# A hybrid decoder layer on one core: convolution sides in parts, attention chunks in three steps, PSUM banks of the output projection in turn, matmuls on a tile of ones at the start

## The chip, the cores and the metric

The kernel runs on one core of a Trainium2 chip. The metric is the device time of one execution in microseconds (us), compared as medians of runs. TensorE (PE) multiplies, VectorE (DVE) and ScalarE (ACT) do the elementwise work, GpSimd (POOL) takes a few reciprocal roots, SyncE's queue (SP) issues nearly all loads and stores.

## What is computed

One layer of a hybrid decoder on 2048 tokens behind 16 learned meta tokens, width 1024, in float32:

```python
s = layer_norm(concat([meta, x]), ln_in_g, ln_in_b)
u = s @ w_in          # columns: conv value, conv gate, q, k, v, r, g_down
c_val, c_gate, q, k, v, r, g_down = split(u)
h = c_val * sigmoid(c_gate)
conv_out = silu(layer_norm(causal_depthwise_conv(h, conv_w, width=31) + conv_b))
log_g = log_sigmoid(g_down @ gate_up + gate_bias) / 16
o = gla_chunked(q, k, v, log_g)     # 4 heads, chunks of 64, state S
gla_out = rms_norm(o, gla_norm_g) * silu(r)
mix = concat([conv_out, gla_out]) @ w_out
s = layer_norm(alpha * s + mix)
s = layer_norm(alpha * s + square(relu(s @ w_ff1)) @ w_ff2)
return s[:, 16:]
```

## The kernel before

The 2048 tokens go through in four sub-sequences of 512 (`NSUB`), each held as four tiles of 128 (`TT`). Every product of float32 matrices is three matmuls of a high and a low part in fp32r (L387-L389, L465-L467, L863-L865, L1013-L1015, L1241-L1243); the splits are a cast on ACT (L190) and a subtraction on DVE (L191).

**Stages.** `win_units(0..3)` project one sub-sequence each with `w_in` (to about 572 us of the profiled execution): gate and value of the convolution, v, the gate's low-rank part (`gd_unit`), r, then two units of K and two of Q. `wout_units(0)` and `(1)` follow to about 720 us, then the two feed-forward products of the first half of the tokens: FF1 (`w1`, to about 1040 us) and FF2 (`w2`, to about 1350 us), both with seven products in place of eight, so that blocks of weights and activations are first added on DVE (L984, L1057, L1191). `wout_units(2)` and `(3)` and the same two products for the second half make up the rest. FF2 writes some added blocks to DRAM (`td<-wr`) and reads them back (`wr<-td`).

**What sets the order.** `Program` holds a list of units, each with an estimated cost. Work beside the units is a generator (a side) with a number of steps, a first and a last unit: `emit` advances it by the share of the cost gone by, and finishes it at its last unit. A scheduler then lays each engine's instructions in order by priority; `later(gen, 100)` lowers that of the convolution, so that its instructions fill gaps. In the trace each engine starts its instructions in that order.

**Convolution.** `conv(s)` loads 512 channels in four blocks (`hin`), starts each on ACT (L720) and adds 30 taps on DVE (L723, one instruction per tap, 480 in all); then for each 128 tokens it transposes (L730), normalises (L732-L742), transposes back (L747), multiplies (L755) and stores to DRAM (`mixd<-cy`, L756). `mix_load(s)` later loads that back (`mraw<-mixd`, L828) and splits it for `wout_units(s)`. Before, `conv(2)` spans from the projections of sub-sequence 3 to the start of FF2, and `conv(3)` lies within FF2.

**Attention.** `gla(s)` runs in seven steps per chunk of 128 tokens: scores (L655, L657), masked copy (L661), state update and output (L667-L680), squares (L687) and their root (L214 on DVE, L215 on POOL), the scaled product `og` with r (L696), four transposes of `og` on PE (L701), copy (L703), store (L704).

**Output projection.** `wout_units` makes two passes of 512 columns, each over four PSUM tiles for the four tiles of 128 tokens: two of the pool `gl` (two banks), two of `mm` (four banks). DVE adds each to `wacc` (L870), which is loaded by `acc_load` (L836).

**End.** The last product of FF2 adds each tile to its sum (`acc1`, L1212), then squares (L240), normalises (L250, L252) and stores.

## Time and profile before

| what | value |
|---|---|
| median of 3 runs | 2082.47 us (2079.40 to 2083.93) |
| profiled execution | 2085.16 us, of which the span 2083.4 us |
| mean granted TensorE clock | 0.992 |
| PE busy | 2022.4 us, 97% |
| DVE busy | 1600.7 us, 77% |
| ACT busy | 1031.5 us, 50% |
| POOL busy | 83.8 us, 4% |
| DMA | 409 MB, 196 GB/s over the span |

The profile is one execution; its times count from the start of the span. Busy time overlaps on PE, because matmuls are pipelined: an instruction of 0.39 us can start 0.23 us after the one before it. A view of waits names an engine, the line that waited, and the instruction that released it.

### The profile page before, as it was taken

The numbers are of one execution on the slowest core, as the hardware profiler recorded it, in microseconds if no ns is written. First come the engines' busy times: TensorE is split into PE (matmuls) and PEld (weight loads), VectorE is DVE, ScalarE is ACT, GpSimd is POOL, SyncE is SP. The second block draws the span as 40 slices with busy tenths as digits, with TensorE's granted clock in tenths as the row PEclk, the third lists the DMA queues.
The fourth block names the chain that finished last, engine by engine and source line by source line (L and its number), as shares of the span: only waits on it lengthen the run. The fifth ranks groups of instructions, "written<-read, shape, count | busy, mean of one in ns | idle before, by whom it ended". The sixth has DMA issues, their size and how long they took to land.

```text
span 2083.4 us, 26276 instructions
## 1 busy us (share of the span) xinstructions
PE 2022.4 (97%) x9144; PEld 1649.9 (79%) x9144; DVE 1600.7 (77%) x2570; ACT 1031.5 (50%) x1774; POOL 83.8 (4%) x97
## 2 busy tenths in 40 slices
PE   7999999999989999999999999999999999999998
PEld 5878778888877878778888788878788788888886
DVE  6699899989997677665598999669877654744776
ACT  4453483554543466555653433545655555444332
POOL 2000000101000000000000000002000000000001
PEclk9999999999999999999999999999999999999999
DMA  6533434434345656654799968367666546965772
GB/s 210 176 98 107 138 112 119 155 104 122 95 149 179 204 189 213 216 187 157 253 337 384 316 233 289 101 213 229 226 222 207 190 149 240 356 225 189 245 246 79
DMA packets 245861, 409.39 MB, mean 196 GB/s; under 512 B 21488, under 2 KB 115920, under 8 KB 245728
## 3 DMA queue, kind: packets, MB, share of 16 engines
q1 hardware_dynamic: 226720, 368.91, 53.8%
q10 hardware_dynamic: 19008, 38.81, 4.9%
q8 instruction: 72, 1.18, 0.2%
q14 instruction: 61, 0.50, 0.1%
HBM read 297.29 MB, written 110.35 MB: 196 GB/s over the span
## 4 chain that ended last, share of the span: by engine, by line
PE 52%; DVE 23%; DMA 14%; issue 4%; ACT 4%; SPq 1%; POOL 1%; ACTq 0%; DVEq 0%; POOLq 0%
DVE cacc L723 8%; PE mm L1241 7%; PE mm L1242 7%; PE mm L1243 7%; DMA w1r<-in_w_dram 5%; PE mm L1013 5%; PE mm L1014 4%; PE mm L1015 4%; DVE wsl L191 2%; DMA lr<-hor 2%; DVE op L191 2%; PE mm L388 2%; PE mm L387 2%; PE mm L389 2%; PE gl L1015 1%
## 5 line engine op out<-in xcount | busy, mean ns | idle before, releaser
L723 DVE SCALAR_TENSOR_TENSOR cacc<-hin,sm,cacc 128x512 f32<-128x512 f32 x480 | 345.1, 744 | 2.7 <-ACT cacc L720 0.9
L190 ACT CAST wsl<-raw 128x512 fp32r<-128x512 f32 x224 | 136.6, 620 | 174.9 <-PE mm L467 53.5
L1242 PE MATMUL mm<-op 128*128 128x512 f32 x544 | 212.5, 391 | 1.6 <-DVE op L191 1.6
L1241 PE MATMUL mm<-op 128*128 128x512 f32 x544 | 212.4, 391 | 0.2 <-DVE ac L1254 0.2
L1243 PE MATMUL mm<-op 128*128 128x512 f32 x544 | 212.2, 390 | 0.0
L190 ACT CAST op<-wr 128x1024 fp32r<-128x1024 f32 x92 | 92.2, 1049 | 210.5 <-PE mm L1243 148.4
L191 DVE TENSOR_TENSOR wsl<-raw,wsl 128x512 fp32r<-128x512 f32 x224 | 150.7, 684 | 29.5 <-ACT wsl L190 29.0
L191 DVE TENSOR_TENSOR op<-wr,op 128x1024 fp32r<-128x1024 f32 x92 | 108.6, 1218 | 69.5 <-ACT op L190 69.4
L191 DVE TENSOR_TENSOR wop<-w1r,wop 128x512 fp32r<-128x512 f32 x152 | 103.2, 687 | 70.6 <-ACT wop L190 69.5
L1013 PE MATMUL mm<-x,wop 128*128 128x512 f32 x384 | 151.7, 396 | 5.3 <-ACT u L1073 4.2
L387 PE MATMUL mm<-xt,wsl 128*128 128x512 f32 x384 | 153.7, 400 | 1.9 <-DVE r L522 1.9
L1014 PE MATMUL mm<-x,wop 128*128 128x512 f32 x384 | 150.7, 392 | 0.6 <-DVE x L191 0.6
L388 PE MATMUL mm<-xt,wsl 128*128 128x512 f32 x384 | 151.2, 394 | 0.0
L389 PE MATMUL mm<-xt,wsl 128*128 128x512 f32 x384 | 150.8, 393 | 0.0
L1015 PE MATMUL mm<-x,wop 128*128 128x512 f32 x384 | 150.4, 392 | 0.0
L191 DVE TENSOR_TENSOR op<-lr,op 128x1024 fp32r<-128x1024 f32 (+1 forms) x96 | 105.1, 1129 | 22.7 <-ACT op L190 22.6
L1242 PEld LDWEIGHTS mm<-op 128*128 128x128 f32 x544 | 102.1, 188 | 23.9 <-DVE op L191 2.8
L1241 PEld LDWEIGHTS mm<-op 128*128 128x128 f32 x544 | 102.1, 188 | 21.8 <-DVE ac L1254 0.6
L1243 PEld LDWEIGHTS mm<-op 128*128 128x128 f32 x544 | 102.1, 188 | 21.4
L190 ACT CAST wop<-w1r 128x512 fp32r<-128x512 f32 x152 | 92.8, 619 | 47.0 <-DVE w1r L984 23.6
L1013 PE MATMUL mm<-xt,wop 128*128 128x512 f32 x256 | 100.7, 396 | 2.9 <-ACT a L1063 2.8
L1013 PE MATMUL gl<-x,wop 128*128 128x512 f32 x256 | 101.4, 396 | 0.0
(278 smaller groups left out, 4781.8 us busy)
## 6 DMA issues: line engine op xcount, KB each, us to landing
wr<-in_w_dram SPq DMA_DIRECT2D x120, 512.0 KB, 6.3
lr<-hor SPq DMA_DIRECT2D x104, 512.0 KB, 6.1
raw<-in_w_in_dram SPq DMA_DIRECT2D x160, 256.0 KB, 3.0
w1r<-in_w_dram SPq DMA_DIRECT2D x64, 512.0 KB, 4.6
wr<-td SPq DMA_DIRECT2D x40, 512.0 KB, 5.5
raw<-in_w_out_dram SPq DMA_DIRECT2D x64, 256.0 KB, 3.8
hor<-s SPq DMA_DIRECT2D x64, 256.0 KB, 3.7
raw<-in_w_dram SPq DMA_DIRECT2D x40, 256.0 KB, 3.9
```

The source lines that it names most:

```text
L190: nc.scalar.copy(hi, src)
L191: (eng or nc.vector).tensor_tensor(out=lo, in0=src, in1=hi.bitcast(F32), op=ALU.subtract)
L387: nc.tensor.matmul(ps, wh, mov(k, 0), start=(k == 0), stop=False)
L388: nc.tensor.matmul(ps, wh, mov(k, 1), start=False, stop=False)
L389: nc.tensor.matmul(ps, wl, mov(k, 0), start=False, stop=(k == KD - 1))
L723: nc.vector.scalar_tensor_tensor(out=acc, in0=h[:, j:j + SUB], scalar=wc(j), in1=acc, op0=ALU.mult, op1=ALU.add)
L1013: nc.tensor.matmul(ps, wh, X[i][:, k, 0, :], start=start and k == 0, stop=False, skip_group_check=not start)
L1014: nc.tensor.matmul(ps, wh, X[i][:, k, 1, :], start=False, stop=False, skip_group_check=not start)
L1015: nc.tensor.matmul(ps, wl, X[i][:, k, 0, :], start=False, stop=(k == 3), skip_group_check=not start)
L1241: nc.tensor.matmul(ps, lh, rt[n][:, p, 0, :], start=(q == 0 and p == 0), stop=False)
L1242: nc.tensor.matmul(ps, lh, rt[n][:, p, 1, :], start=False, stop=False)
L1243: nc.tensor.matmul(ps, ll, rt[n][:, p, 0, :], start=False, **ends)
```

## The change

Six edits:

1. A tile of ones and 22 bf16 matmuls of 128x512 on it stand ahead of the first transposes.
2. `conv(2)` and `conv(3)` are one chain of steps: 49 between the start of `wout_units(0)` and the start of FF1, 148 from 24 units into FF1 to the start of FF2, 99 within FF2.
3. `gla` has three steps per chunk, and the transposes, the copy and the store of a chunk's `og` are issued in the first step of the next chunk (`turn`).
4. The passes of `wout_units` take their PSUM tiles by turns as `ggmm`, `mmgg`, `mmmm`.
5. In the projections of sub-sequence 3, `mix_load(0)` is added between the two Q units and no longer ahead of the K units.
6. The last `acc1` of the second half has a higher priority.

```diff
 from contextlib import ExitStack
+from itertools import chain
 import numpy as np
...
             s.finish()
+def part(gen, n):
+    for _ in range(n):
+        try:
+            next(gen)
+        except StopIteration:
+            return
+        yield
 @with_exitstack
 def hymba_kernel(ctx: ExitStack, tc: tile.TileContext, x, meta, ln_in_g, ln_in_b, w_in, small, gate_up,
                  w_out, ln1_g, ln1_b, w1, w2, ln2_g, ln2_b, out):
...
     nhalf = cpool.tile([P, NH], F32, name="nhalf")
     nc.vector.memset(nhalf, -0.5)
     sm = cpool.tile([P, SM_N], F32, name="sm")
+    ones = cpool.tile([P, P], BF16, name="ones")
+    nc.vector.memset(ones, 1.0)
+    wm = glp.tile([P, 512], F32, tag="gl", name="gl").rearrange("p (a c) -> p a c", a=4)
+    for _ in range(22):
+        nc.tensor.matmul(wm, ones, ones.rearrange("p (a c) -> p a c", a=1).broadcast_to([P, 4, P]), start=True, stop=True)
     s0d = [[dp.tile([P, D], F32, name=f"s0d{s}_{t}") for t in range(TT)] for s in range(NSUB)]
     hd = [[dp.tile([P, HALO + SUB], F32, name=f"hd{s}_{c}") for c in range(CT)] for s in range(NSUB)]
...
         w.gd = prog.mark()
         prog.add(gd_unit, cost=4.5)
         tok_units(C_R, r_evac, True)
+        for u in ch_units(C_K, k_evac, km_evac if s == 0 else None):
+            prog.add(*u)
+        qu = ch_units(C_Q, q_evac)
+        prog.add(*qu[0])
         if s == NSUB - 1:
             prog.add(lambda: mix_load(0), cost=0.01)
-        for u in ch_units(C_K, k_evac, km_evac if s == 0 else None):
-            prog.add(*u)
-        for u in ch_units(C_Q, q_evac):
-            prog.add(*u)
+        prog.add(*qu[1])
     def gla(s):
         w = W[s]
+        out_ = [None]
+        def turn():
+            if out_[0] is None:
+                return
+            og, lo = out_[0]
+            tp = tp_tile()
+            for h in range(NH):
+                nc.tensor.transpose(tp[:, h * P:(h + 1) * P], og[:, h * P:(h + 1) * P], ident)
+            go = pa.tile([P, 512], F32, tag="go", name="go", bufs=1)
+            nc.scalar.activation(go, tp, AF.Identity, scale=sm[:, SM_GG:SM_GG + 1])
+            nc.sync.dma_start(out=mixd[s][1][:, :, lo:lo + P], in_=go.rearrange("p (h t) -> p h t", h=NH))
+            out_[0] = None
         for c in range(TT):
             a = gl_tile().rearrange("p (h c) -> p h c", h=NH)
             lo, hi = c * P, c * P + CH
...
                                  start=True, stop=True)
                 nc.tensor.matmul(a[:, 2 * p:2 * p + 2, CH:], w.kx[p][:, lo:lo + P], qbd[p][:, :, hi:hi + CH],
                                  start=True, stop=True)
-            yield
+            turn()
             ats = at[c % 2]
             nc.vector.copy_predicated(ats, msk.bitcast(I32).rearrange("p (a c) -> p a c", a=1)
                                       .broadcast_to([P, NH, P]), a)
...
             for h in range(NH):
                 nc.tensor.matmul(o[:, h * P:(h + 1) * P], ats[:, h, :], w.v[c][:, h * P:(h + 1) * P],
                                  start=False, stop=(h == NH - 1))
-            yield
             for p in range(2):
                 for h in range(2):
                     rows, cols = slice(h * 64, (h + 1) * 64), slice(h * P, (h + 1) * P)
                     nc.vector.scalar_tensor_tensor(out=sout[rows, p, cols], in0=sin[rows, p, cols],
                                                    scalar=w.e[p].dt[rows, c:c + 1], in1=ds_[rows, p, cols],
                                                    op0=ALU.mult, op1=ALU.add)
-            yield
             og = pa.tile([P, 512], F32, tag="og", name="og")
             ss = stp.tile([P, NH], F32, tag="ss", name="ss")
             for h in range(NH):
...
                 sl = slice(h * P, (h + 1) * P)
                 nc.vector.scalar_tensor_tensor(out=og[:, sl], in0=o[:, sl], scalar=rr[:, h:h + 1],
                                                in1=w.r[c][:, sl], op0=ALU.mult, op1=ALU.mult)
-            yield
-            tp = tp_tile()
-            for h in range(NH):
-                nc.tensor.transpose(tp[:, h * P:(h + 1) * P], og[:, h * P:(h + 1) * P], ident)
-            go = pa.tile([P, 512], F32, tag="go", name="go", bufs=1)
-            nc.scalar.activation(go, tp, AF.Identity, scale=sm[:, SM_GG:SM_GG + 1])
-            nc.sync.dma_start(out=mixd[s][1][:, :, lo:lo + P], in_=go.rearrange("p (h t) -> p h t", h=NH))
-            yield
-
-    GLA_N = TT * 7
+            out_[0] = (og, lo)
+            yield
+        turn()
+        yield
+    GLA_N = TT * 3 + 1
     hdone = set()
...
             a = wacc[s, tt] = B.w.tile([P, D], F32, tag="wacc", name="wacc", bufs=4)
             nc.sync.dma_start(out=a, in_=s0d[s][tt])
+    turns = [0]
     def wout_units(s, late=None):
         sums = {}
...
             def unit(k, c=c, ls=ls, st=st):
                 if k == 0:
-                    st.ps = [gl_tile() if tt < 2 else mm_tile() for tt in range(TT)]
+                    st.ps = [(gl_tile if x == "g" else mm_tile)() for x in ("ggmm", "mmgg", "mmmm")[turns[0] % 3]]
+                    turns[0] += 1
                 wsl = prog.slot[ls[k]]
                 for tt in range(TT):
                     xh = xs(mx[s], k, 0)[:, tt * P:(tt + 1) * P]
...
                 add(x.slot[5], x.slot[5], x.slot[7])
             else:
                 o, to = {2: (x.c[:, 0], x.sa[:, 0:1]), 3: (x.c[:, 1], x.sa[:, 1:2]), 4: (x.c[:, 2], x.sb[:, 0:1])}[i]
-                acc1(o, o, ps, 1.0, to)
+                with tc.high_priority(offset=60 if half and i == 4 else 0):
+                    acc1(o, o, ps, 1.0, to)
                 if half and i == 4:
                     for _ in ln2(3, tt):
                         pass
...
     prog.side(gla(NSUB - 1), GLA_N, m_wout - 1, m_wout)
     prog.side(later(conv(0), CONV_LATE), CONV_N, W[0].gv_end, bounds[1] + 16)
     prog.side(later(conv(1), CONV_LATE), CONV_N, W[1].gv_end, bounds[3])
-    prog.side(later(conv(2), 100), CONV_N, W[3].gv_end, m_f20)
-    prog.side(later(conv(3), 100), CONV_N, m_f20, m_w2 - 4)
+    both = chain(later(conv(2), 100), later(conv(3), 100))
+    n_a, n_b = CONV_N // 3, CONV_N
+    prog.side(part(both, n_a), n_a, m_wout + 2, m_ff0 - 6)
+    prog.side(part(both, n_b), n_b, m_ff0 + 24, m_f20)
+    prog.side(both, 2 * CONV_N - n_a - n_b, m_f20, m_w2 - 4)
     prog.side(ln2_sub(0), 3 * TT, m_w2, m_w3)
     prog.side(ln2_sub(1), 3 * TT, m_w3, m_ff1)
     prog.emit()
```

Line numbers of the changed kernel are higher: L214 is L231 there, L191 is L208, L696 is L728, L680 is L713, L723 is L751, L1191 is L1223, L756 is L784, L787 is L815, L828 is L856, L836 is L864.

On DVE, in the projections of sub-sequence 1, where `og` of the third chunk of `gla(0)` is made, there stands before (`rr` is the root of the mean square, `wsl` and `xt` are splits for the projection):

```order
L191 TENSOR_TENSOR wsl<-raw,wsl 128x512
L191 TENSOR_TENSOR xt<-tp,xt 128x4x128 x2
L214 TENSOR_SCALAR rr<-ss 128x4
L723 SCALAR_TENSOR_TENSOR cacc<-hin,sm,cacc 128x512
L696 SCALAR_TENSOR_TENSOR og<-gl,rr,r 128x128
L723 SCALAR_TENSOR_TENSOR cacc<-hin,sm,cacc 128x512
L191 TENSOR_TENSOR wsl<-raw,wsl 128x512
L723 SCALAR_TENSOR_TENSOR cacc<-hin,sm,cacc 128x512
L696 SCALAR_TENSOR_TENSOR og<-gl,rr,r 128x128
```

and in the changed kernel:

```order
L713 SCALAR_TENSOR_TENSOR S_279<-S_278,dt,gl 64x128 x4
L231 TENSOR_SCALAR rr<-ss 128x4
L208 TENSOR_TENSOR wsl<-raw,wsl 128x512
L208 TENSOR_TENSOR xt<-tp,xt 128x4x128 x2
L728 SCALAR_TENSOR_TENSOR og<-gl,rr,r 128x128 x4
L751 SCALAR_TENSOR_TENSOR cacc<-hin,sm,cacc 128x512
L208 TENSOR_TENSOR wsl<-raw,wsl 128x512
L751 SCALAR_TENSOR_TENSOR cacc<-hin,sm,cacc 128x512 x3
```

The four L696 stand together, without taps between them. On PE the four transposes that read them were one by one between the matmuls; they are one group now, whose first stands 57 matmuls later.

On DVE in FF2 of the first half, from the third sum `wr<-wr` of added blocks on (`op` and `ox` are split operands, of loads `wr` and `lr`), there stands before:

```order
L1191 TENSOR_TENSOR wr<-wr 128x1024
L191 TENSOR_TENSOR op<-wr,op 128x2x512 x2
L191 TENSOR_TENSOR op<-lr,op 128x2x512 x2
L723 SCALAR_TENSOR_TENSOR cacc<-hin,sm,cacc 128x512
L1191 TENSOR_TENSOR wr<-wr 128x1024
L723 SCALAR_TENSOR_TENSOR cacc<-hin,sm,cacc 128x512 x7
L191 TENSOR_TENSOR ox<-wr,ox 128x2x512 x2
L191 TENSOR_TENSOR op<-lr,op 128x2x512 x2
L723 SCALAR_TENSOR_TENSOR cacc<-hin,sm,cacc 128x512
L1191 TENSOR_TENSOR wr<-wr 128x1024
L723 SCALAR_TENSOR_TENSOR cacc<-hin,sm,cacc 128x512
```

and in the changed kernel:

```order
L1223 TENSOR_TENSOR wr<-wr 128x1024
L208 TENSOR_TENSOR op<-wr,op 128x2x512 x2
L208 TENSOR_TENSOR op<-lr,op 128x2x512 x2
L1223 TENSOR_TENSOR wr<-wr 128x1024 x2
L208 TENSOR_TENSOR ox<-wr,ox 128x2x512 x2
L208 TENSOR_TENSOR op<-lr,op 128x2x512 x2
L1223 TENSOR_TENSOR wr<-wr 128x1024 x2
L208 TENSOR_TENSOR op<-wr,op 128x2x512 x2
L208 TENSOR_TENSOR op<-lr,op 128x2x512 x2
```

The taps (L723) between the splits and the added blocks are gone from this stretch. The other taps of `conv(3)` stand earlier, in FF1, and further on in FF2.

On SP ahead of `wout_units(2)`, from the second store of `conv(3)` on (`g`, `b` belong to the following normalisation), there stands before:

```order
L756 DMA mixd_0_238<-cy 512x1x128
L828 DMA mraw<-mixd_1_237 128x512 x2
L756 DMA mixd_0_238<-cy 512x1x128 x2
L787 DMA g_11722<-in_ln_g_dram 128x1024
L787 DMA b_11724<-in_ln_b_dram 128x1024
L828 DMA mraw<-mixd_0_238 128x512 x4
L836 DMA wacc<-s0d_0_100 128x1024
L828 DMA mraw<-mixd_1_239 128x512 x4
L836 DMA wacc<-s0d_1_101 128x1024
L836 DMA wacc<-s0d_2_102 128x1024
L836 DMA wacc<-s0d_3_103 128x1024
```

and in the changed kernel:

```order
L784 DMA mixd_0_263<-cy 512x1x128
L856 DMA mraw<-mixd_0_261 128x512 x4
L856 DMA mraw<-mixd_1_262 128x512 x4
L784 DMA mixd_0_263<-cy 512x1x128 x2
L815 DMA g_11747<-in_ln_g_dram 128x1024
L815 DMA b_11749<-in_ln_b_dram 128x1024
L856 DMA mraw<-mixd_0_263 128x512 x4
L864 DMA wacc<-s0d_0_125 128x1024
L856 DMA mraw<-mixd_1_264 128x512 x4
L864 DMA wacc<-s0d_1_126 128x1024
L864 DMA wacc<-s0d_2_127 128x1024
L864 DMA wacc<-s0d_3_128 128x1024
```

The last two stores of `cy` are still ahead of `g` and `b`; the eight loads for sub-sequence 2 stand together behind the second store, where six of them stood ahead of it.

## Rows read from the trace of the kernel before

**Rows 1.** The page's part 1: busy time, share of the span, instructions.

```profile
PE 2022.4 (97%) x9144; PEld 1649.9 (79%) x9144; DVE 1600.7 (77%) x2570; ACT 1031.5 (50%) x1774; POOL 83.8 (4%) x97
```

**Rows 2.** Waits of PE: engine, line, releaser: us in total, times, longest.

```profile
PE tp L261 <- DVE xin L252: 10.4, 4, 9.2
PE mm L1242 <- DVE op L191: 6.0, 4, 4.3
PE tp L701 <- DVE og L696: 5.7, 5, 3.7
...
PE tp L571 <- DVE e L565: 3.6, 2, 2.8
PE gl L863 <- DVE wacc L870: 3.1, 3, 1.8
...
PE mm L387 <- DVE r L522: 1.9, 1, 1.9
...
PE gl L863 <- ACT wsl L190: 0.8, 1, 0.8
```

**Rows 3.** Timeline of PE to 18.54 us, then PE's groups in 18.3 to 23.

```profile
14.47 0.63 PE L465 MATMUL mm<-wsl,xt 128*128 128x512 f32 x1
...
17.88 0.59 PE L467 MATMUL mm<-wsl,xt 128*128 128x512 f32 x1
18.31 0.40 PE L465 MATMUL mm<-wsl,xt 128*128 128x512 f32 x1
18.54 0.40 PE L466 MATMUL mm<-wsl,xt 128*128 128x512 f32 x1
...
L465 PE MATMUL mm<-wsl,xt 128*128 128x512 f32 x5 | 2.1, 414 | 1.2 <-ACT xt L190 1.2
```

**Rows 4.** Timeline of 229 to 235: start, length, engine, line, tile, [idle before].

```profile
234.56 0.45 PE L701 MATMUL tp<-ident,og 128*128 128x128 f32 x1 [3.71 <-DVE og L696]
```

**Rows 5.** Windows: length, busy PE, PEld, DVE, ACT, POOL, granted clock, DMA share, GB/s.

```profile
233.00:241.00 8.00, 6.44 (x23) 5.35 (x24) 6.01 (x13) 1.77 (x3) 1.03 (x1) 0.57 0.29 100
```

**Rows 6.** Timeline of DVE at the K units of sub-sequence 3.

```profile
575.48 1.88 DVE L191 TENSOR_TENSOR xt<-mraw,xt 128x512 fp32r<-128x512 f32 x3
...
581.19 0.42 DVE L565 TENSOR_TENSOR e<-e,d 128x256 f32<-128x256 f32 x1
```

**Rows 7.** Groups of DVE in 964 to 984.5 (busy, mean ns, idle before), one FF1 group.

```profile
L191 DVE TENSOR_TENSOR wop<-w1r,wop 128x512 fp32r<-128x512 f32 x6 | 4.1, 684 | 2.4 <-ACT wop L190 2.3
...
L1057 DVE TENSOR_TENSOR p<-p,mm 128x512 f32<-128x512 f32 x2 | 1.4, 689 | 5.9 <-PE mm L1015 5.9
```

**Rows 8.** Windows of FF1 and FF2, columns as in rows 5.

```profile
960.00:1000.00 40.00, 40.00 (x182) 32.66 (x181) 24.44 (x44) 24.18 (x43) 1.41 (x2) 1.00 0.49 171
...
1072.00:1096.00 24.00, 24.00 (x107) 19.87 (x107) 24.00 (x27) 8.87 (x10) 0.00 (x0) 1.00 0.84 293
...
1120.00:1144.00 24.00, 23.47 (x104) 19.12 (x103) 18.73 (x20) 8.27 (x9) 0.00 (x0) 1.00 1.03 407
...
1169.00:1176.00 7.00, 6.18 (x16) 4.88 (x17) 7.00 (x9) 1.77 (x3) 0.00 (x0) 0.54 0.88 289
```

**Rows 9.** Timelines of DVE in FF2, 1064 to 1070 and 1150 to 1171.

```profile
1064.78 4.72 DVE L723 SCALAR_TENSOR_TENSOR cacc<-hin,sm,cacc 128x512 f32<-128x512 f32 x7
...
1167.40 1.23 DVE L1191 TENSOR_TENSOR wr<-wr 128x1024 f32<-128x1024 f32 x1 [4.16 <-DMA wr<-td]
```

**Rows 10.** Waits of SP's queue in 1340 to 1390, then its timeline, then a window.

```profile
SPq L756 <- DVE cy L755: 21.7, 2, 13.6
...
1374.34 12.51 SPq L200 DMA_DIRECT2D raw<-in_w_out_dram  x7
...
1380.00:1388.00 8.00, 7.23 (x20) 5.10 (x20) 7.36 (x16) 4.62 (x8) 1.70 (x2) 0.57 0.54 188
```

**Rows 11.** The chain of waits at the end: start, length, what.

```profile
2074.07 1.41 DVE ac L252 x2
2075.48 0.61 DVE ac L1212 x2
```

## The prediction

> **What bounds the kernel now.** I read the page's busy times first: PE is busy for 2022.4 of 2083.4 us [rows 1]. So 61 us are all that idle time can give back, and what lies before the first product and behind the last one is part of that. Next I read PE's waits by their cause [rows 2]: each is short, most are for DVE, which is busy for 1600.7 us and starts its instructions one behind the other. Then the windows with their granted clock: where PE waited long in one go, the clock stands near half afterwards (0.57 over 233 to 241 us [rows 5], 0.54 over 1169 to 1176 [rows 8], 0.57 over 1380 to 1388 [rows 10]), that is, at the lower of its levels, 1.2 GHz, for most of the stretch. A long wait is paid twice: while PE stands, and then at half speed. The change adds no work worth speaking of except at the start; it moves work on DVE and SP. So the question for each part is which of these waits it ends, and what stands in the way next.
>
> **Matmuls at the start.** Until 17.88 us the matmuls start 0.43 us apart, from 18.31 on 0.23 [rows 3]: the first pace is that of the lower level. From 14.47 to 18.31 nine of them follow one another (3.84 / 0.43), which at the faster pace would save 9 x 0.20 = 1.8 us. But the very next groups wait 1.2 us for ACT's split of activations [rows 3], so data are late there anyway. The 22 added matmuls cost at most 22 x 0.43 = 9.5 us from about 1 us on, and the first transposes come at 9.2, when PE's first wait ends [rows 2], so they are at worst 1.3 us late. Bounds -1.8 and +1.3; I take **-0.5**, nearest to the row of the following wait. The Trainium skill ("TensorE: Matmul & The Clock Gate", "Why this matters for your kernels") advises warming up with matmuls before others are measured, and the pace in rows 3 agrees that the first ones are slow; by that rule alone this term would be -1.8.
>
> **Attention in three steps.** In the third chunk of `gla(0)` PE stands 3.71 us at the first transpose, since `og` is late [rows 4]. Then come eight microseconds at a mean clock of 0.57 [rows 5]: 8 x (1 - 0.57) x 2 = 6.9 us at half speed, less the 1.56 us until PE starts again, so 5.3 us of work done at half speed, a loss of 2.7. In the order of the changed kernel the transposes stand 57 matmuls later, 57 x 0.23 = 13 us, long after `og` is made. Both losses go: -6.4. The copies and stores of a chunk come later by one chunk, too; they are read only by the output projection, a stage later. What is next on PE is the r product of the same sub-sequence: `mm L387 <- DVE r L522` waits 1.9 us [rows 2], and in the new order the gate's exponentials and r's evacuation stand 2 us or so (four taps of 0.7 us at most, 3 us) further back on ACT and DVE. That price is +2, between 0 and +3. Sum **-4.4**; bounds -6.4 and, if the r wait grows by 3 and the clock falls after it for 2.7 in the same way, -0.7.
>
> **Projection operands behind the keys.** PE waits 2.8 us at the transposes of the keys for L565 [rows 2]; its queue holds splits of `mraw` on DVE from 575.48 to 581.19 [rows 6]. Moving the load takes six such splits of 0.63 us, 3.8 us, from ahead of L565, but in the new order four or five taps stand in this gap instead, 0.66 us apart (seven within 4.72 us [rows 9]), some 3 us. SP issues the eight loads behind those for the K units, and the splits come behind the keys; `wout_units(0)` needs them only after `gla(3)`, which hides that, or costs up to 1 if it does not. Gain between -1 and 4.5 (the 2.8 and 1.7 of a fallen clock after it, estimated from the 2.7 after the wait of 3.7); I take **-0.6**, about the 0.8 that is left of 3.8 less 3.
>
> **Banks in turn.** Of the three waits of the output projection for its evacuation, 3.1 us in all, the longest is 1.8 and lies in `wout_units(2)` [rows 2]; the other two, 1.3 us, come where the second pass needs the tiles of the first. With free `mm` banks for two of four tiles, and more in later passes, they go: **-1.3**, bounds -1.3 and 0.
>
> **Convolution in parts, FF1.** In 960 to 1000 DVE is busy for 24.4 of 40 us [rows 8], or 12.5 of the 20.5 us of a group; about 1.2 of it is the end of `conv(2)`, which the new order has earlier. It puts 12 to 15 taps into each of four groups up to 1040: 11.3 + 14 x 0.66 = 20.5. DVE is full, then, and its waits of 2.4 us for ACT and 5.9 us for PE [rows 7] are no longer slack that the others can use freely. The price lies between 0, if the taps fall just into those 8.3 us, and 4 x 2.4 = 9.6, if each wait for ACT comes on top. I take **+1.0**, near the lower end, because the 5.9 us wait is for PE itself and moves with it.
>
> **Convolution in parts, FF2.** Here is the largest item. PE waits 6.0 us for splits, 4.3 of it in one go [rows 2], and runs at a mean clock of 0.54 afterwards: 7 x (1 - 0.54) x 2 = 6.4 us, a loss of 2.8 net of the 0.8 us that PE idles [rows 8]. Total 8.8. The long wait ends behind a sum of blocks (L1191) that itself waited 4.16 us for a load, `wr<-td` [rows 9]. So it looks like a DMA limit. But earlier, in 1072 to 1096, DVE is busy for all 24 us while the DMA engines are busy for 0.84 and move 293 GB/s; in 1120 to 1144 they move 407 [rows 8]. In the first stretch buffers came free too late, because 32 taps stand among the splits up to 1104 in the order of before, and 9 after: 23 x 0.66 = 15 us of DVE gone. If the engines then move 407 in place of 293, they are (407 - 293) x 24 = 2.7 MB, or 6.7 us, ahead, which covers 6.0 us of waits. Bounds: -8.8, and -2 if the waits for loads stay and only the short ones go. I take **-7**. The Trainium skill ("DMA: Bandwidth & Descriptors", "Where 436 GB/s comes from") puts the HBM limit of a core at about 358 GB/s; the 407 of rows 8 is above that, so the row decides. By the page the lead would be (358 - 293) x 24 / 358 = 4.4 us, an estimate, and the term about -4.4.
>
> **Convolution in parts, second output projection.** Before `wout_units(2)` SP's queue waits 21.7 us for the last two `cy` [rows 10]; only then come the last loads of operands and the weights (from 1374.34). PE's waits there are 1.8 and 0.8 us [rows 2], and the clock afterwards is 0.57 over 8 us, 6.9 us at half speed, about 3.1 us lost: 5.7 in all. In the new order the taps of `conv(3)` end some 50 us earlier, so the last `cy` are bound by PE's transposes alone, which stand right ahead of the projection and not 24 matmuls into it (24 x 0.23 = 5.5 us earlier). That exceeds the 2.6 us of waits. Against it: two loads of `mraw` more stand behind the second store. I take **-5.5**, bounds -5.7 and -1.
>
> **Last sum first.** `acc1` of the last tile starts at 2075.48, behind L252 twice (1.41 us from 2074.07) [rows 11]. Ahead of them, it and the square after it start up to 1.9 us earlier, but the same 1.41 us of DVE then stand behind it: **-0.6**, bounds -1.9 and 0.
>
> **Sum.** -0.5 - 4.4 - 0.6 - 1.3 + 1.0 - 7.0 - 5.5 - 0.6 = -18.9. From the profiled execution, 2085.16, that gives 2066.3; from the median of the runs, 2082.47, which lies 2.7 lower, 2063.6. I predict between them, **2065**.
>
> **Rivals.**
> - *DVE is full and the waits only move.* In the projections and FF1 a tap lands in front of the next needed instruction. For it: the 24.00 of 24 us in rows 8 and the taps in place of the splits at 577. The terms of attention and FF2 halve, 5.7 less, and FF1 costs 4 in place of 1, near the middle of its bounds: 2065 + 5.7 + 3 = **2074**.
> - *FF2 is bound by its loads.* For it: 1.03 and 407 GB/s in 1120 to 1144. Then only -2 of FF2 is left, 2065 + 5 = **2070**.
> - *FF1 becomes bound by DVE (slower).* In each of four groups from 964 to 1040 DVE waits 2.4 us for ACT with a tap of 0.7 behind or ahead, and PE waits for the sum after it. If PE stands 3.1 us in one go, it then also loses some 2.7 to the clock, as after the 3.7 us at 230: 4 x 5.8 = 23 in place of 1, so 2065 + 22 = **2087**. From 4.6 us a group on (18.5 / 4) the kernel is slower than before. Against it: 5.9 us of DVE's idle time there are waits for PE.
> - *The change does not reach what it moves*, because other waits of the same length stand right behind: **2081**.
> - *All favourable bounds*: -1.8 - 6.4 - 4.5 - 1.3 - 8.8 - 5.7 - 1.9 with FF1 at 0 is -30.4, so **2053**.
>
> **How the numbers follow.** Forecast with its neighbourhood and the FF2 rival: 0.58; DVE full: 0.17; favourable bounds: 0.08; does not reach: 0.10; slower: 0.07. A measurement of this kernel tells about 0.2%, 4.2 us, from no change. Faster by more: the first three, 0.83, and little of the fourth, together 0.84. Within 0.2%: 0.09. Slower: 0.07. The range leaves out the slower rival and the outermost favourable cases: 2053 to 2082.
>
> **What would show it.** Right: no wait of PE over 1 us at the transposes of `og` in 225 to 260, and clock 1.00 there; no 4 us wait in FF2, over 380 GB/s in 1072 to 1096; clock 1.00 around `wout_units(2)`. Wrong: PE waits for DVE's sums in 960 to 1040; a wait over 3 us at the r product; the wait for `wr<-td` unchanged; the transposes at the start later than 9.2.

## The result and the profile after

The changed kernel takes 2071.15 us (median of 6 runs, 2066.82 to 2075.0) against 2082.77 for the kernel before (6 runs): a ratio of 0.9943, 95% interval 0.9927 to 0.9958, 11.6 us faster. Measured again beside other kernels it was 2069.01 against 2084.39, 0.9922 (0.9910 to 0.9935). Its profiled execution took 2066.82 us (span 2065.1) and is the fastest of the six, while that of before, 2085.16, lies above all six of its runs: of the 18.3 us between the two spans 6.7 come from this choice of executions (18.3 - 11.6).

The page's part 1, to be read beside [rows 1]:

```profile
PE 2016.9 (98%) x9166; PEld 1643.4 (80%) x9166; DVE 1602.1 (78%) x2571; ACT 1034.1 (50%) x1774; POOL 84.6 (4%) x97
```

PE is 5.5 us less busy, though it does more (the matmuls on ones take 6.5 us): it runs less at the lower clock. Its waits, as in [rows 2] (engine, line, releaser: us in total, times, longest):

```profile
PE tp L278 <- DVE xin L269: 4.0, 4, 1.8
...
PE tp L588 <- DVE e L582: 3.0, 2, 2.2
...
PE gl L689 <- ACT qbd L566: 2.7, 2, 2.1
PE mm L404 <- DVE r L539: 2.5, 1, 2.5
...
PE mm L895 <- DVE wacc L902: 1.9, 2, 1.7
PE mm L1273 <- DVE ac L1286: 1.8, 2, 1.3
PE tp L679 <- DVE og L728: 1.6, 2, 0.9
...
PE mm L1274 <- DVE op L208: 1.2, 1, 1.2
```

The two long ones of before are gone: 4.3 us for FF2's splits (the longest of that line is now 1.2, at FF2's start) and 3.7 us for `og` (now 0.9). Four of about 2 us have come or grown: `xin`, `qbd`, `r`, and the evacuation `wacc` on an `mm` bank. Windows, columns as in [rows 5]:

```profile
226.00:234.00 8.00, 7.75 (x40) 6.65 (x41) 7.82 (x18) 2.83 (x5) 1.39 (x1) 1.00 0.57 197
...
573.00:582.00 9.00, 9.00 (x43) 7.40 (x42) 9.00 (x16) 5.25 (x10) 0.00 (x0) 1.00 0.63 200
...
1152.00:1159.00 7.00, 7.00 (x33) 5.79 (x32) 4.43 (x4) 1.98 (x5) 0.00 (x0) 1.00 1.04 412
...
1382.50:1412.00 29.50, 28.48 (x137) 22.31 (x138) 27.81 (x61) 14.05 (x24) 4.25 (x5) 1.00 0.67 216
```

They are at the place of the old `og` transposes, behind the keys, at the place of the old wait for FF2's splits, and in `wout_units(2)`. The granted clock is 1.00 in all of them, where [rows 5], [rows 8] and [rows 10] had 0.54 to 0.57. In the last one DVE is busy for 27.81 of 29.50 us.

Where the time went is best seen from the same products of PE in both traces. The table gives, for products that start at a given time in the kernel before, how much earlier (-) or later they start in five other profiled executions:

| us in before | changed | changed, again | only conv | only gla | changed without conv |
|---|---|---|---|---|---|
| 104 | 0.0 | +1.1 | +1.7 | +1.6 | +1.4 |
| 120 | -2.2 | -1.1 | +1.5 | -0.7 | -0.8 |
| 225 | -2.6 | -1.5 | +1.5 | -1.0 | -1.2 |
| 260 | -6.9 | -6.2 | +2.1 | -5.5 | -3.5 |
| 545 | -7.8 | -7.7 | +2.1 | -5.1 | -4.4 |
| 600 | -9.7 | -8.9 | +1.6 | -5.8 | -6.2 |
| 660 | -9.1 | -9.5 | +1.8 | -5.4 | -6.6 |
| 1042 | -9.4 | -9.4 | +5.4 | -1.6 | -9.2 |
| 1180 | -17.8 | -17.0 | -1.9 | -6.8 | -13.1 |
| 1356 | -15.5 | -14.3 | -0.6 | -5.0 | -12.4 |
| 1390 | -21.7 | -20.3 | -7.0 | -4.5 | -14.7 |
| 1453 | -17.9 | -16.6 | -3.5 | -4.5 | -12.9 |
| 2072 | -17.8 | -18.5 | -5.1 | -4.6 | -10.7 |

Steps in it are stages: 104 to 120 is a place behind the first gates that the prediction does not name (below), 225 to 260 the attention, 545 to 600 the keys, 1042 to 1356 FF2, 1356 to 1453 the output projections. At the end, 0.5 us more come from the last sum (18.3 in the span).

### The profile page after: what moved, and what is told of

Its sections match the earlier page's. It is cut to its first block, busy times and chain, and to the rows that moved or that the text cites. A ratio compares the mean times of both kernels' runs of the same rounds, so it can differ in the third digit from the quotient of the medians.

```text
span 2065.1 us, 26307 instructions
## 1 busy us (share of the span) xinstructions
PE 2016.9 (98%) x9166; PEld 1643.4 (80%) x9166; DVE 1602.1 (78%) x2571; ACT 1034.1 (50%) x1774; POOL 84.6 (4%) x97
## 4 chain that ended last, share of the span: by engine, by line
PE 49%; DVE 23%; DMA 17%; ACT 5%; issue 4%; SPq 1%; POOL 1%; ACTq 0%; DVEq 0%; POOLq 0%
DVE cacc L751 7%; DMA w1r<-in_w_dram 6%; PE mm L1275 5%; PE mm L1273 5%; PE mm L1274 5%; PE mm L1045 5%; PE mm L1046 4%; PE mm L1047 4%; DMA wr<-td 2%; PE mm L405 2%; PE mm L406 2%; PE mm L404 2%; DVE wsl L208 2%; DVE op L208 2%; DMA wr<-in_w_dram 2%
## 5 line engine op out<-in xcount | busy, mean ns | idle before, releaser
L751 DVE SCALAR_TENSOR_TENSOR cacc<-hin,sm,cacc 128x512 f32<-128x512 f32 x480 | 348.0, 745 | 6.9 <-ACT cacc L748 3.7
L208 DVE TENSOR_TENSOR wsl<-raw,wsl 128x512 fp32r<-128x512 f32 x224 | 150.6, 685 | 25.2 <-ACT wsl L207 25.0
L208 DVE TENSOR_TENSOR op<-wr,op 128x1024 fp32r<-128x1024 f32 x92 | 108.8, 1220 | 76.4 <-ACT op L207 76.3
L208 DVE TENSOR_TENSOR wop<-w1r,wop 128x512 fp32r<-128x512 f32 x152 | 103.0, 687 | 56.5 <-ACT wop L207 55.6
L208 DVE TENSOR_TENSOR op<-lr,op 128x1024 fp32r<-128x1024 f32 (+1 forms) x96 | 105.1, 1129 | 11.8 <-ACT op L207 11.8
```

The source lines that it names most:

```text
L208: (eng or nc.vector).tensor_tensor(out=lo, in0=src, in1=hi.bitcast(F32), op=ALU.subtract)
L751: nc.vector.scalar_tensor_tensor(out=acc, in0=h[:, j:j + SUB], scalar=wc(j), in1=acc, op0=ALU.mult, op1=ALU.add)
```

## Experiments

**Three parts alone.** Each is the kernel before with one edit of the change.

```diff
 # only_gla: turn() and three steps per chunk
-    GLA_N = TT * 7
+    GLA_N = TT * 3 + 1
 # only_conv
...
+    prog.side(part(both, n_a), n_a, m_wout + 2, m_ff0 - 6)
+    prog.side(part(both, n_b), n_b, m_ff0 + 24, m_f20)
+    prog.side(both, 2 * CONV_N - n_a - n_b, m_f20, m_w2 - 4)
 # only_banks
+                    st.ps = [(gl_tile if x == "g" else mm_tile)() for x in ("ggmm", "mmgg", "mmmm")[turns[0] % 3]]
```

> Only the attention in three steps of the changed kernel. Theory (each edit ends its own wait): the 3.7 us wait at the transposes of og near 234 us and the low clock behind it go (-6.4), the wait at the r product grows, so about -4.5 us against the kernel before, with the 4 us wait in FF2 and the low clock near 1380 us still there. Rival (DVE is full, waits move): a wait of over 2.5 us comes back within 100 us and the clock falls after it in most executions; -1 us or less.

> Only the convolution in parts. Theory: FF2's long wait goes (-7), FF1 costs 1 to 3, the second output projection gains 2 to 5: -6 to -9 us. Rival (the waits of FF2 are for loads and went by chance in one execution): 4 us wait for the load behind wr<-td still there, no more than -2 us. Second rival (FF1 bound by DVE): waits of PE for DVE or ACT in 890 to 1040 add over 6 us and the sum is 0.

> Only the PSUM banks of the output projection in turn. Theory of the prediction: the 1.05 us wait in wout_units(0) and the 1.8 us one in wout_units(2) go, -1.3 to -3 us. Rival: in turns of mmmm the pass takes all four mm banks, the next one waits for its evacuation, and a new wait of 1.5 us or more stands in wout_units(2): 0 us in the sum.

Measured against the kernel before on the same chip (2084.16 us): attention 0.9982 (0.9971 to 0.9994), convolution 0.9983 (0.9970 to 0.9996), banks 1.0006 (0.9993 to 1.0019). By these ratios that is 3.8 us, 3.5 us and nothing. The attention does what the theory says (-4.5 from 225 to 260 in the table); in that profile it has another -2.3 at 104 to 120, where its edit changes nothing, and loses 3.8 from 660 to 1042. The convolution alone gains 6.0 in FF2 and 2.9 in the output projections, but loses 3.6 from 660 to 1042, nearly all of it in FF1: near the theory's parts, but under its sum of 6 to 9. The banks gain nothing. From the list of PE's waits in the whole of that execution (FF1, FF2, and in the last line `wout_units(2)`):

```profile
PE mm L1031 <- ACT u L1091: 6.0, 10, 1.4
...
PE mm L1260 <- DVE op L203: 5.2, 3, 3.9
...
PE mm L881 <- DVE wacc L888: 2.3, 1, 2.3
```

The wait for `wacc` is 2.3 us on `mm` in place of 1.8 on `gl` [rows 2]: other banks do not end it. FF2's wait is there, 3.9 us, as it should be with the old order of taps.

**The change without the convolution, and once more.**

```diff
 # no_conv, against the changed kernel
-    both = chain(later(conv(2), 100), later(conv(3), 100))
...
+    prog.side(later(conv(2), 100), CONV_N, W[3].gv_end, m_f20)
+    prog.side(later(conv(3), 100), CONV_N, m_f20, m_w2 - 4)
```

> The changed kernel with the convolution placed as before. Theory: the wait of about 4 us in FF2 for the block behind wr<-td and the low clock after it come back, and so do the waits at the start of wout_units(2): 4 to 8 us slower than the changed kernel. Rival (FF2's wait comes and goes with the time at which the stage is reached): no wait over 2 us in FF2, and within 2 us of the changed kernel.

> The changed kernel once more, for a second profiled execution and on the same chip as the three others. If the gains are those of its order of instructions, the waits at the transposes of og near 230 us and in FF2 near 1155 us are gone again, and its median is 11 to 12 us below the kernel before. If the 18 us between the two first profiles were luck of one execution, the lower clock or the waits stand in other places here, and the profile lies some 5 us higher.

Without the convolution the ratio is 0.9946 (0.9932 to 0.9959), 2074.88 us, against 0.9922 for the changed kernel beside it: 5.9 us between the medians, within the theory's 4 to 8. But the wait in FF2 that came back is 1.9 us and not 4:

```profile
PE mm L1274 <- DVE op L208: 3.0, 3, 1.9
```

In the eight executions with the old order of taps the longest wait of PE in that place was 4.3 (before), 3.9, 3.4, 1.9, 1.9, 1.8, 1.8 and 1.2 us. With the new order five of six have none over 0.2 us there (the changed kernel twice, only_conv, no_warm_last, conv_earlier); evac_first2, which moves other things too, has 1.3. The profile of before showed a long one. Over the same stretch of FF2, to this wait, before, changed and without the convolution:

```profile
1048.00:1170.00 122.00, 116.56 (x511) 95.38 (x510) 111.27 (x122) 48.80 (x56) 0.00 (x0) 0.99 0.97 356
```

```profile
1040.00:1155.00 115.00, 115.00 (x509) 95.25 (x508) 97.56 (x98) 48.67 (x55) 0.00 (x0) 1.00 0.99 371
```

```profile
1039.00:1158.00 119.00, 116.80 (x514) 95.84 (x513) 111.08 (x121) 48.36 (x56) 0.00 (x0) 1.00 0.97 359
```

The first and third have 24 and 23 instructions more on DVE. The DMA engines were busy for 0.97 in before, too; 0.99 and 371 GB/s are what the shorter stretch gives. PE is now busy all through.

**The matmuls on ones.** The changed kernel without them (and without the priority of the last sum), they alone, and three probes of why:

```diff
 # no_warm_last: both edits taken out of the changed kernel; only_warm: the kernel before, with
+    for _ in range(22):
+        nc.tensor.matmul(wm, ones, ones...broadcast_to([P, 4, P]), start=True, stop=True)
...
 # warm_one
+    for _ in range(1):
 # warm_even: one matmul on a first gl tile, 21 on a second
+    wm = glp.tile([P, 512], F32, tag="gl", name="gl").rearrange("p (a c) -> p a c", a=4)
 # warm_short
+        nc.tensor.matmul(wm[:, :16], ones, ones[:, :16], start=True, stop=True)
```

> The changed kernel without the matmuls on the tile of ones and without the priority of the last sum. Theory of the prediction: 0.5 and 0.6 us are missing, so about 1 us slower than the changed kernel (2072 against 2071). Rival: the clock that rises during the matmuls on ones falls again before the first products, so only the transposes gain 0.2 us, and the kernel is the same as the changed one.

> Only the matmuls on the tile of ones at the start. Theory of the prediction: -0.5 us. Rival 1: the clock rises during them, falls again in the gaps of the first transposes, and the first products run at the lower level as before: 0 us. Rival 2: the first 20 us gain nothing, but the clock no longer falls near 114 us behind the 1.1 us wait there, as in the first profile of the changed kernel: -2 to -4 us.

> The kernel before with one matmul on the tile of ones in place of 22: next to no work at the start, but its PSUM tile takes one of the two gl banks, so every later gl tile lies in the other bank than before; the order of the other instructions is the same. Theory (the gain of the 22 matmuls comes from the banks): the wait at L379 near 113 us is 0.5 and not 1.1 us, the one at the transposes of og near 234 us 2.8 and not 3.7, and the time is 3 to 6 us below the kernel before. Rival (it comes from the clock at the start): 0 us.

> The kernel before with 22 matmuls on ones, one of them on a first gl tile and 21 on a second, so that every later gl tile lies in the same bank as before. Theory (banks): the wait near 113 us is 1.1 us again, that near 234 us 3.7, and the time is that of the kernel before. Rival (clock at the start): 3 to 6 us below, as with 22 on one tile.

> The kernel before with 22 matmuls on the tile of ones that have 16 columns each in place of 512: as many instructions on PE ahead of the transposes, but about 1 us of work in place of 7, so the clock should stay at its lower level until the first products. Theory (the gain of 0.2 to 0.3% with 22 long matmuls comes from PE's work at the start): 0 us, as with one matmul. Rival (it comes from 44 more instructions in PE's stream, which move later ones against whatever fetches them): 3 to 6 us below the kernel before, and small waits for ACT in FF1 of the first half, 1 to 3 us in all and not 3 to 5.

| kernel | ratio to before | 95% interval |
|---|---|---|
| changed, without ones and last sum | 0.9962 | 0.9949 to 0.9975 |
| 22 matmuls of 512 columns | 0.9973 | 0.9960 to 0.9986 |
| the same, later banks as before | 0.9981 | 0.9971 to 0.9992 |
| 22 matmuls of 16 columns | 0.9983 | 0.9971 to 0.9995 |
| 1 matmul of 512 columns | 1.0007 | 0.9996 to 1.0017 |

By these ratios 22 matmuls alone gain 3.5 to 5.6 us, more than the prediction's widest bound, and one gains nothing. It is not gained at the start: in the changed kernel the first products still run 0.43 us apart up to 18.1 us. PE's timeline, and its windows:

```profile
1.15 6.49 PE L184 MATMUL gl<-ones 128*128 128x512 bf16 x22 [1.15 <-DVE ones L181]
9.08 1.32 PE L278 MATMUL tp<-ident,xin 128*128 128x128 f32 x8 [1.44 <-DVE xin L269]
12.00 0.79 PE L482 MATMUL mm<-wsl,xt 128*128 128x512 f32 x1 [1.60 <-ACT xt L207]
...
17.32 0.63 PE L483 MATMUL mm<-wsl,xt 128*128 128x512 f32 x1
17.75 0.53 PE L484 MATMUL mm<-wsl,xt 128*128 128x512 f32 x1
18.11 0.40 PE L482 MATMUL mm<-wsl,xt 128*128 128x512 f32 x1
```

```profile
9.00:14.00 5.00, 2.79 (x11) 1.60 (x12) 5.00 (x11) 3.28 (x6) 3.07 (x7) 0.72 0.97 357
14.00:18.00 4.00, 4.00 (x10) 3.13 (x11) 3.97 (x10) 2.47 (x4) 0.85 (x1) 0.50 0.72 211
18.00:23.00 5.00, 3.76 (x18) 2.93 (x18) 3.67 (x7) 2.51 (x5) 0.13 (x1) 1.00 0.73 160
```

22 matmuls in 6.49 us is a mean of 0.30, between the paces of 0.43 and 0.23, so the clock rose among them. Behind the waits of 1.44 and 1.60 us it is at 0.72 over 9 to 14 and at 0.50 over 14 to 18. The banks theory falls with warm_one and warm_even, and the clock theory with warm_short, whose matmuls take under a microsecond:

```profile
1.15 0.75 PE L184 MATMUL gl<-ones 128*128 128x16 bf16 x22 [1.15 <-DVE ones L181]
9.43 1.97 PE L278 MATMUL tp<-ident,xin 128*128 128x128 f32 x8 [7.53 <-DVE xin L269]
```

What the three kernels that gain have in common is 44 more instructions on PE ahead of everything else (22 matmuls and 22 weight loads; warm_one has 2 more and gains nothing), with the order of all the others unchanged. One place where they gain can be shown. Near 114 us PE stands at a matmul of the gates for `hm` (`gl<-i,um`, L379 of before). Before, and the changed kernel:

```profile
113.47 0.39 PE L379 MATMUL gl<-i,um 32*128 32x16 f32 x2 [1.13 <-DVE hm L619]
```

```profile
112.86 0.39 PE L396 MATMUL gl<-i,um 32*128 32x16 f32 x2 [0.50 <-DVE hm L636]
```

and the windows of 8 us around it, again before and changed:

```profile
112.00:120.00 8.00, 6.87 (x28) 5.54 (x26) 5.99 (x11) 3.16 (x6) 0.00 (x0) 0.79 0.37 103
```

```profile
112.00:120.00 8.00, 7.50 (x38) 6.14 (x37) 7.52 (x14) 4.37 (x8) 0.00 (x0) 1.00 0.33 95
```

38 matmuls in place of 28. In the five executions of kernels without the 22 matmuls other than only_gla (before, only_conv, only_banks, no_warm_last, warm_one) this wait is 0.91 to 1.15 us, and the clock falls behind it in four of them; in all eight with the 22, long or short, and in only_gla it is 0.50 us, and the clock falls in none. From 104 to 120 us the eight and only_gla gain about 2.2 us on before, only_banks 1.6, and the other three 0.3 at most. So about half of the gain shows there.

What sets this wait can be followed back in the traces. On DVE `hm` stands behind a tap and the split `gd` (L394 of before), and `gd` behind another tap. `gd` can start as soon as ACT's cast for it is done, if the tap ahead of it is done by then; in the eight and in only_gla it is, in the other five the split is 0.4 to 0.65 us late. The order on DVE is the same up to 188 us in all of them; what differs is when the taps of `conv(0)` begin. ACT starts the convolution behind its work on `xin`, and SP issues the loads for both (`xin`, `hin`) behind two small stores, `hd<-hm`. The DMA queue 8, which the profile calls `instruction`, and these stores in 84 to 87.6 us, before (packets, MB, share of the engines; KB each, us to landing):

```profile
q8 instruction: 1, 0.02, 2.1%
...
hd<-hm SPq DMA_DIRECT2D x2, 15.0 KB, 2.9
```

and changed, where queue 8 moves nothing in that stretch:

```profile
hd<-hm SPq DMA_DIRECT2D x2, 15.0 KB, 1.5
```

Queue 8 moves 72 packets of 16 KB in a run, about one for every 254 instructions of PE and PEld (18288 before). In the six executions without the 22 matmuls one packet starts at 84.6 to 86.4 us, beside these stores, which land after 2.3 to 2.9 us; in all eight with them the same packet comes at 80.4 to 82.1 us, ahead of the stores, which land after 1.5. The store of `xin` at 61 to 63 us shows the same: 4.6 to 5.2 us in the six, with a packet at 62 to 65, and 2.7 in the eight, whose packet comes at 56 to 58. At 31 us it is the other way round: there the packet falls beside the store in the eight, which take 4.5 to 5.0 us, and later in the six, which take 2.6 to 2.9. So 44 instructions move these packets against the stores, and 2 (warm_one, packet at 84.7) do not. That a packet slows a store is read from these coincidences, without an exception in 14 executions; no run moves a packet alone. only_gla has the slower stores too (2.3 and 2.4 us), but its taps are just early enough.

Where the rest of the gain lies is open. Some may be in FF1 of the first half: between the products that start at 725 and 930 us in before, PE idles for 3.3 us in before, 3.7 to 5.0 in the other kernels without 22 long matmuls, 2.1 to 2.6 with those alone, 1.6 in no_conv and 1.2 to 1.3 in the changed kernel, both times (5.9 and 6.9 in the two kernels of the next part, which move more work there). But warm_short, at 3.7, gains without it.

**Two attempts at a faster version.**

```diff
 # conv_earlier
-    n_a, n_b = CONV_N // 3, CONV_N
+    n_a, n_b = CONV_N // 2, CONV_N
 # evac_first2: around the evacuations of wout_units and of FF1's products
+            with tc.high_priority(offset=60):
+                nc.scalar.copy(nxt_b[-1], src)
```

> The changed kernel with 74 in place of 49 of the convolution's steps beside the first two output projections, and 74 in place of 99 left for FF2. If the two waits for sums near 1200 and 1207 us (1.8 us) come from the taps in FF2 and DVE has room beside the output projections (21 of 30 us busy), 1 to 3 us faster than the changed kernel. If the taps delay the evacuations there or FF1's sums, 0 to 4 us slower.

> The changed kernel with a higher priority (60) for the evacuations of the output projection and of FF1's products on ACT and DVE. If the waits that are left in FF1 (a and u, 6 us in both halves) and at the third output projection (1.7 us) come from splits that stand ahead of the evacuations, 3 to 6 us faster than the changed kernel. If they come from the time at which the splits arrive, splits are later instead and the time is the same or up to 4 us longer.

conv_earlier has 0.9939 (0.9926 to 0.9952), no better than the changed kernel. PE's two waits for `ac` in FF2 near 1200 us, 0.3 to 1.6 and 1.3 us in the other executions with the new order of taps, are gone from its trace (under 0.2), but the transposes at the end of `conv(2)` now stand in PE's queue where ACT and POOL have not normalised yet:

```profile
PE tp L775 <- ACT cn L770: 5.2, 3, 4.4
```

and the clock falls behind the longest of these waits, 4.4 us:

```profile
882.00:889.00 7.00, 6.38 (x21) 4.92 (x22) 1.69 (x3) 4.02 (x9) 0.00 (x0) 0.57 0.82 265
```

So the gain at 1200 is spent at 880. evac_first2 is slower than the changed kernel by 0.7% (0.9988, 0.9976 to 0.9999):

```profile
PE mm L1047 <- DVE p L1092: 14.2, 16, 1.5
```

PE now waits 16 times for DVE's sums in the FF1 of both halves, 14.2 us in all; the changed kernel has one such wait in the whole run, of 0.9. That the evacuations put first on ACT hold up the splits, and these DVE, would explain it, but no run tests that.

## Why the prediction was right, and where it was not

The time lay within the range (2071.15 in 2053 to 2082), and its direction is clear of no change; the forecast of 2065 took 17.5 us off, and 11.6 and 15.4 were measured. So the direction and the order of size were right, and two thirds of the forecast gain came, or a little more beside the other kernels. That the sum, -18.9, came out almost exactly in the profile (-18.3) is luck: errors cancel, and 6.7 us of the 18.3 are the choice of executions. Term by term, forecast and then measured in the two profiles of the changed kernel. The last column is steadier: over the 12 executions of all kernels but conv_earlier and evac_first2, the mean of those with the edit less the mean of those without it, between the same products:

| term | forecast | two profiles | with less without |
|---|---|---|---|
| start | -0.5 | 0.0 and +1.1 at 104 us, -2.2 at 104 to 120 | alone -3.5 to -5.6 by ratio |
| attention | -4.4 | -4.3, -4.7; alone -3.8 by ratio | -3.0 |
| keys | -0.6 | -1.9, -1.2; 0.6 of the first given back by 660 | -1.3 |
| banks | -1.3 | 0 | 0 |
| FF1 | +1.0 | +2.3 (changed less no_conv, 660 to 1042); alone +3.6 | +0.8 |
| FF2 | -7.0 | -6.1, -4.9; of it the taps 2.9, 1.7 | -2.9 |
| output projection 2 | -5.5 | -2.4, -2.3 | -2.5 |
| last sum | -0.6 | -0.5 | -0.65 |

*Attention: right in the mechanism, by another route, and on average smaller.* The wait and the low clock went, -6.4, as said. The r wait did not grow by 2: it is 2.5 for 1.9 [rows 2], and 2.0 to 2.8 in all executions with the new steps against 1.9 to 2.8 with the old. Instead the transposes of the next inputs, `xin`, wait there at 226 us: 1.4 to 2.1 us in all seven executions with the new steps, 0.3 at most in the other seven. Behind the two longest of these waits (2.1 us, no_conv and no_warm_last) the clock fell, and only 2.3 and 3.0 were gained. Of the seven with the old steps, one (only_warm, wait 2.8) kept its clock and was 3.6 faster there than before. So the -6.4 is what one execution of before had to lose; on average it is about 3.

*Keys: direction right, size about twice the forecast.* The taps filled the gap, as forecast, and 2.2 us of the 2.8 stayed. What the working left out is that 0.6 us less of a wait can spare the whole fall of the clock behind it. With the load moved the wait was 2.0 to 2.2 us in five executions of six, and the clock fell behind it in none; with the old order it was 2.8 to 3.4 us in eight, and fell in six. In those other two, and in the sixth with the load moved (conv_earlier), waits of 3.0 to 3.1 us cost no clock, so this is a matter of odds. A part comes back 17 us later, where PE waits for `qbd` 2.0 to 2.4 us in all six with the load moved and 2.0 at most in the other eight. The edit was not run alone; this is read from traces.

*FF2: the mechanism was right, the profile of before a bad sample.* Its 4.3 us was the longest of eight executions with that order of taps. DVE is relieved early in the stage as said, 16.66 us busy of 24 in place of 24.00 [rows 8]:

```profile
1062.00:1086.00 24.00, 24.00 (x108) 19.88 (x107) 16.66 (x15) 9.45 (x11) 0.00 (x0) 1.00 0.93 322
1110.00:1134.00 24.00, 24.00 (x108) 19.87 (x107) 21.77 (x24) 8.27 (x9) 0.00 (x0) 1.00 1.04 410
```

The step that failed is "the engines then move 407 in place of 293": here they moved 322, and over the whole stretch 371 in place of 356. The sign of over 380 GB/s in 1072 to 1096 did not come either (335). It was enough to end the wait, and DVE's own wait for `wr<-td` there is 1.4 us in place of 4.16 [rows 9]:

```profile
DVE wr L1223 <- DMA wr<-td: 3.6, 4, 1.4
```

But the taps are worth only the smaller waits that are usual there: the executions with the old order of taps are 2.7 us faster in FF2 than that of before, on average over all eight, and the four with the new order (conv_earlier and evac_first2 left out) 5.7.

*Second output projection: the step that failed was to stop the sum at 1390.* Up to there the gain is 6.2 and 6.0 us, more than forecast. Then 3.8 and 3.7 are given back by 1453, of it 2.5 and 2.4 as idle time of PE. DVE was full there before:

```profile
1402.00:1430.00 28.00, 28.00 (x140) 23.07 (x139) 27.45 (x59) 13.99 (x24) 4.61 (x5) 1.00 0.69 230
```

PE now arrives earlier at a bank whose evacuation stands behind DVE's other work. On DVE, at that point:

```profile
1380.66 0.68 DVE L208 TENSOR_TENSOR wsl<-raw,wsl 128x512 fp32r<-128x512 f32 x1
1381.27 0.74 DVE L269 SCALAR_TENSOR_TENSOR ac<-ac,rs,b 128x512 f32<-128x512 f32 x1
1381.93 0.68 DVE L902 SCALAR_TENSOR_TENSOR wacc<-wacc,mm 128x512 f32<-128x512 f32 x1
```

and PE behind it:

```profile
1382.67 0.50 PE L895 MATMUL mm<-wsl,xt 128*128 128x512 f32 x1 [1.70 <-DVE wacc L902]
```

only_conv and no_warm_last give back 3.5 and 3.7 in the same stretch, with their waits for `wacc` at other points of it. That is the rival "DVE is full and the waits only move", in a place that its text did not name.

*Banks: the term is nothing.* The step that failed is "with free `mm` banks for two of four tiles they go": the wait is for DVE's evacuation, and it went along to the other bank.

*FF1: no wall of waits.* The slower rival asked for PE to stand for sums in four groups; over 940 to 1040 it stands once:

```profile
PE mm L1045 <- DVE p L1089: 0.9, 1, 0.9
```

*Start: the mechanism failed.* The step that failed is that the added matmuls leave the faster pace to the products from 14.47 us on: the clock did not stay up, so the first 20 us gain nothing. The gain that the matmuls bring lies elsewhere and is larger; that this term's sign was right is luck. The -1.8 that the prediction worked out by the Trainium skill ("TensorE: Matmul & The Clock Gate", "Why this matters for your kernels") came no more than the forecast's -0.5.

*Last sum: right.* It was not run alone either; from the last product to the end of the span the five executions with it gain 0.5 to 0.8 us on before, and the eight others without it 0 or lose up to 0.3.

## What to carry to other kernels

A wait of 2 to 4 us on the busiest engine is worth up to about twice its length, because the clock may fall behind it; but read its length from several executions before pricing it, since the same order gave 1.2 to 4.3 us in one place. When a wait goes, follow the engine that is fullest in the next two stages: here 2.4 of the 6.2 us that the output projection gained were left after it. The four parts run alone, without the moved load and the last sum, multiply to 0.9982 x 0.9983 x 1.0006 x 0.9973 = 0.9944, and the whole measured 0.9943 and 0.9922. Each factor is known to about 0.0013 only, so this fits, but does not prove that the parts add up. A profile shows one execution: where several kernels share a stage, compare all of them there before giving a gain to an edit.

## What was not expected of the hardware

- 22 matmuls at the very start, even of 16 columns and 0.75 us in all, made the kernel 0.17 to 0.27% faster; one did nothing (1.0007). It is neither the clock of the first products nor the PSUM bank. About half of it shows near 114 us, behind stores that no longer run beside a packet of the queue `instruction`; the rest stays open. Other counts were not tried.
- Stores beside such a packet of 16 KB landed later in every execution: 2.3 to 2.9 us in place of 1.5 for 15 KB at 84 to 87 us, 4.6 to 5.2 in place of 2.7 for `xin` at 61 to 63.
- The clock fell behind a wait of 0.9 to 1.15 us near 114 us in four of five executions, behind one of 0.5 us in none of nine; yet at the keys waits of 3.0 us left it at 1.00 three times. The length of one wait alone does not tell whether it falls.
- The DMA engines moved 371 GB/s over 115 us and 410 over 24. The Trainium skill ("DMA: Bandwidth & Descriptors", "Where 436 GB/s comes from") puts the HBM limit of a core at about 358 GB/s, half of what it states for a stack that two cores share; these transfers pass it. What the other core did is not on record.
